# Weights-stationary products by halves with all high parts first, and 512-wide recurrence products, in a one-core transformer block

## The chip, the cores and the metric

The kernel runs on one core of one Trainium2 chip. The metric is device time in microseconds from the first to the last instruction of one execution with what lies around it; the kernel before takes 1810.07 us (median of 3 runs, 1809.61 to 1811.19).

## What is computed

One block over 256 tokens of width 2048, in fp32:

```python
mod = silu(c) @ ada_w + ada_b                  # 6 rows of 2048: sh1, sc1, g1, sh2, sc2, g2
h = rmsnorm(x, norm1_g) * (1 + sc1) + sh1
q, kc, vc, ks, vs, kw, vw, g_nsa, lx, ly, ga, gb = split(h @ w_in)
o_a = attention(...)                           # compressed, selected and window branches, gated
u = causal_dwconv(lx, conv_w, conv_b)
o_b = gelu(ly) * rg_lru(u, ...)                # gated linear recurrence over the tokens
merged = sigmoid(ga) * (o_a @ proj_a) + sigmoid(gb) * (o_b @ proj_b)
x = x + g1 * (merged @ w_out)
h = rmsnorm(x, norm2_g) * (1 + sc2) + sh2
gate, val = split(h @ ffn_up)
x = x + g2 * ((gelu(causal_dwconv(gate, ...)) * val) @ ffn_down)
out = rmsnorm(x, final_g)
```

## The kernel before

**Split products.** A product in fp32 accuracy is made of fast fp32r products. Each operand is split in a high part (rounded) and a low part (the rest), and three products are summed: high x high, high x low, low x high. Activations are kept split, `[:, 0:256]` high and `[:, 256:512]` low for the 256 tokens. Weights are streamed: a piece of 128 x 2048 (1 MB) is loaded on SP's queue into one of four `raw` buffers (`stage`), and each half of it (1024 columns) is split by `split`: ScalarE copies the high part (L107), VectorE subtracts to get the low part (L108). There are three buffers each for high and low halves, and both instructions have raised priority.

**Three product forms.** In `dense_tok` the activations are stationary and the weights move, 512 wide (L202 to L204): gates of the merge, output projections, `w_out` and the FFN's down product. In the other forms the weights are stationary. `dense_pair` gives two blocks of 128 outputs (f = 0, 1), each in a PSUM bank of its own. For each of the eight weight blocks of a half, high weights multiply the whole 512 columns of the split activations (L130), so that the bank's two halves hold high x high and high x low, and low weights then multiply the 256 high columns (L131). `reduce` (L226, VectorE) adds the bank's two halves at the end. The FFN's up products use it, 42 calls with two pieces each. `dense_pair1` keeps both blocks in one bank and issues three products of 256 columns per weight block (L184, L186, L187), which add up in place; no reduction is needed. It is used for the recurrence's inputs (8 calls, a ScalarE copy at L670 after each) and its gates (8 calls, a Gelu at L721 that reads the bank). All forms take their banks from the same four PSUM banks `d`.

**Stages.** Modulation of the first norm and the attention inputs come first (to about 290 us of the trace), then attention units interleaved with recurrence inputs (to about 480 us), the recurrence with its gates (to 597), the merge in four blocks n of 512 outputs (to 906), `w_out` (to about 985), and the FFN in two halves of 12 groups of up products and 4 down products each.

**Recurrence.** For each bt of 4, VectorE makes the convolution `u`, TensorE two small products, ScalarE two sigmoids, a tanh, an exp and a square root, VectorE the scan (L707 to L716). Then for h of 2 a gate product runs, its Gelu is written over `u` (L720, L721), multiplied by the scan's result and split into `oB` (L722 to L726).

**Modulation pieces.** The last four of the six modulation rows need 64 pieces of 1 MB. `filler(n)` takes the next n: a load into a `raw` buffer, a multiply with sum on VectorE (L233) and a small addition (L234). They are placed between the products: 2 after each recurrence input, 2 after two of the gate products, 2 after each product pair of the merge's first block and 4 after those of the other three, and 16 in the FFN.

**Order.** Every load keeps program order on SP's queue (`load`, L53). A load waits there until its buffer has been read, and whatever stands behind it on the queue waits too. The order on the engines comes from a planner that simulates the program with its own costs and priorities.

## Time and profile before

| | |
|---|---|
| median of 3 runs | 1810.07 us |
| the profiled execution | 1810.84 us, span 1809.0 us |
| TensorE busy | 1788.1 us, 99% of the span, 10344 matmuls |
| VectorE busy | 1338.8 us, 74% |
| ScalarE busy | 867.3 us, 48% |
| recurrence (480 to 597 us) | TensorE 114.9, VectorE 97.3, ScalarE 87.9 of 117 us |
| merge (597 to 830 us) | TensorE 232.4, VectorE 162.4, ScalarE 98.8 of 233 us, DMA 78% |

A line of a group names the source line, the engine, the operation, output and inputs, the number of instructions, busy time and mean duration, and the idle time of the engine before them. PE is TensorE's matmul side and PEld its weight loads, DVE is VectorE, ACT ScalarE, SPq SP's DMA queue. Matmuls are pipelined: their durations overlap, and the distance from start to start is shorter than a duration.

### The profile page before, as it was taken

Reading aid. Unit: us, or ns where it says so; the run is one execution under the profiler, and the core shown is the slowest. Engines: PE = TensorE matmul, PEld = TensorE weight load, DVE = VectorE, ACT = ScalarE, POOL = GpSimd, SP = SyncE. Lnnn points to the kernel's source line nnn. Section 1 sums busy time; section 2 is a strip of 40 time slices with the busy share of each in tenths; the row PEclk is TensorE's granted clock in tenths of the full one; section 3 lists DMA queues with packets and bytes.
Section 4 is the critical chain, followed back from the end, with each engine's and each line's share of the span. In section 5 each row is a group of like instructions: output and inputs, shape, how many; then the busy total and the mean of one; then the engine's idle time right before and its main releaser. Section 6 shows DMA issues by size and latency. Waiting matters only on the chain.

```text
span 1809.0 us, 25836 instructions
## 1 busy us (share of the span) xinstructions
PE 1788.1 (99%) x10344; PEld 1555.3 (86%) x10344; DVE 1338.8 (74%) x1942; ACT 867.3 (48%) x1176; POOL 0.2 (0%) x4
## 2 busy tenths in 40 slices
PE   8999999999999999999999999999999999999998
PEld 7899898788899888888888998888888888888886
DVE  7999866898788866767666898888555666666555
ACT  5645434655578443434445544444433444444443
POOL 0000000000000000000000000000000000000000
PEclk9999999999999999999999999999999999999999
DMA  9999862666556768787776566777655555555553
GB/s 357 366 333 361 316 245 96 214 227 210 210 175 222 273 241 292 282 285 284 294 278 209 172 231 235 277 279 279 249 190 189 188 189 189 191 190 190 186 189 113
DMA packets 64201, 429.51 MB, mean 237 GB/s; under 512 B 7089, under 2 KB 7377, under 8 KB 15569
## 3 DMA queue, kind: packets, MB, share of 16 engines
q1 hardware_dynamic: 63792, 427.08, 66.3%
q8 instruction: 81, 1.33, 0.3%
q10 hardware_dynamic: 288, 0.79, 0.1%
q14 instruction: 40, 0.32, 0.1%
HBM read 425.72 MB, written 2.11 MB: 237 GB/s over the span
## 4 chain that ended last, share of the span: by engine, by line
PE 94%; DVE 3%; DMA 1%; ACT 1%; issue 1%; DVEq 0%; ACTq 0%
PE P L130 17%; PE P L203 11%; PE P L204 11%; PE P L202 11%; PE P L131 9%; PE P L187 3%; PE P L184 3%; PE P L186 3%; PE P L426 2%; PE P L428 2%; PE P L427 2%; PE P L420 2%; PE P L421 2%; PE P L419 1%; PE P L148 1%; PE P L147 1%
## 5 line engine op out<-in xcount | busy, mean ns | idle before, releaser
L107 ACT ACTIVATE hi<-raw 128x1024 fp32r<-128x1024 f32 x589 | 623.2, 1060 | 808.9 <-PE P L204 322.0
L108 DVE TENSOR_TENSOR lo<-raw,hi 128x1024 fp32r<-128x1024 f32 x589 | 718.6, 1223 | 388.1 <-ACT hi L107 387.1
L130 PE MATMUL P<-h,hi 128*128 128x512 f32 x1344 | 465.9, 397 | 0.0
L131 PE MATMUL P<-h,lo 128*128 128x256 f32 x1344 | 362.8, 280 | 0.0
L130 PEld LDWEIGHTS P<-h,hi 128*128 128x128 f32 x1344 | 246.7, 188 | 53.2
L131 PEld LDWEIGHTS P<-h,lo 128*128 128x128 f32 x1344 | 253.6, 189 | 7.7
L233 DVE SCALAR_TENSOR_TENSOR raw<-raw,crow 128x2048 f32<-128x2048 f32 x64 | 146.3, 2286 | 13.0 <-DMA raw<-ada_w 13.0
L187 PE MATMUL P<-h,lo 128*128 128x256 f32 x512 | 147.1, 288 | 2.1 <-DVE lo L108 2.1
L184 PE MATMUL P<-h,hi 128*128 128x256 f32 x512 | 146.7, 287 | 0.0
L186 PE MATMUL P<-h,hi 128*128 128x256 f32 x512 | 146.6, 286 | 0.0
L426 PE MATMUL P<-h,hi 128*128 128x256 f32 x384 | 108.0, 286 | 0.0
L427 PE MATMUL P<-h,hi 128*128 128x256 f32 x384 | 107.3, 284 | 0.0
L428 PE MATMUL P<-h,lo 128*128 128x256 f32 x384 | 102.2, 284 | 0.0
L187 PEld LDWEIGHTS P<-h,lo 128*128 128x128 f32 x512 | 97.7, 191 | 3.9 <-DVE lo L108 2.6
L184 PEld LDWEIGHTS P<-h,hi 128*128 128x128 f32 x512 | 97.9, 191 | 3.3 <-issue 3.0
L186 PEld LDWEIGHTS P<-h,hi 128*128 128x128 f32 x512 | 97.9, 191 | 1.1 <-issue 1.0
L203 PE MATMUL P<-lo,ua 128*128 128x512 f32 x240 | 93.4, 389 | 0.0
L204 PE MATMUL P<-hi,ua 128*128 128x512 f32 x240 | 93.4, 389 | 0.0
L202 PE MATMUL P<-hi,ua 128*128 128x512 f32 x240 | 83.6, 389 | 0.0
L203 PE MATMUL P<-lo,h 128*128 128x512 f32 x192 | 75.5, 393 | 0.6 <-DVE lo L108 0.5
L204 PE MATMUL P<-hi,h 128*128 128x512 f32 x192 | 74.9, 390 | 0.0
L426 PEld LDWEIGHTS P<-h,hi 128*128 128x128 f32 x384 | 74.1, 193 | 0.2
(265 smaller groups left out, 3121.9 us busy)
## 6 DMA issues: line engine op xcount, KB each, us to landing
raw<-ada_w SPq DMA_DIRECT2D x96, 1024.0 KB, 5.0
raw<-w_up SPq DMA_DIRECT2D x96, 1024.0 KB, 4.9
raw<-w_down SPq DMA_DIRECT2D x48, 1024.0 KB, 4.9
raw<-w_lru SPq DMA_DIRECT2D x32, 1024.0 KB, 5.0
raw<-w_proj SPq DMA_DIRECT2D x32, 1024.0 KB, 5.0
raw<-w_gates SPq DMA_DIRECT2D x24, 1024.0 KB, 6.4
raw<-w_out SPq DMA_DIRECT2D x16, 1024.0 KB, 5.0
raw<-w_kv SPq DMA_DIRECT2D x24, 512.0 KB, 6.8
```

The source lines that it names most:

```text
L107: A.activation(hi[:, :n], raw[:, lo_col:lo_col + n], AF.Copy)
L108: V.tensor_tensor(lo[:, :n], raw[:, lo_col:lo_col + n], hi[:, :n].bitcast(F32), op=ALU.subtract)
L130: PE.matmul(ps[f], hi[:, sl], r, start=(kt == 0), stop=False, skip_group_check=True)
L131: PE.matmul(o, lo[:, sl], r[:, 0:256], start=False, stop=(kt == n - 1), skip_group_check=True)
L184: PE.matmul(o, hi[:, sl], r[:, 0:256], start=(kt == 0 and f == 0), stop=False, skip_group_check=True)
L186: PE.matmul(o, hi[:, sl], r[:, 256:512], start=False, stop=False, skip_group_check=True)
L187: PE.matmul(o, lo[:, sl], r[:, 0:256], start=False, stop=(kt == n - 1), skip_group_check=True)
L202: PE.matmul(ps[j], xh, hi[:, w], start=(kt == 0), stop=False, skip_group_check=True)
L203: PE.matmul(ps[j], xh, lo[:, w], start=False, stop=False, skip_group_check=True)
L204: PE.matmul(ps[j], xl, hi[:, w], start=False, stop=(kt == n - 1), skip_group_check=True)
L233: V.scalar_tensor_tensor(raw, raw, 1.0, row, op0=ALU.mult, op1=ALU.mult, accum_out=modc[:, c:c + 1])
L426: PE.matmul(o, hi[:, sl], h1[:, kt, 0:256], start=first and f % 2 == 0, stop=False, skip_group_check=True)
```

## The change

`dense_pair` now issues, for each half of a piece, the eight products with high weights first (both blocks), and then the eight with low weights. `dense_pair1` is dropped. Recurrence inputs and gates call `dense_pair` in its place: each call takes two banks, and two reductions on VectorE replace the ScalarE copy, or stand ahead of the Gelu, which now reads and writes SBUF. One modulation piece follows each recurrence input in place of two, and the eight pieces so taken out are put into the merge: 3 for 2 after each product pair of its first block, 5 for 4 after those of the other blocks.

```diff
-        def dense_pair(pieces, rhs, narrow=False):
+        def dense_pair(pieces, rhs):
...
                     hi, lo = split(raw, half * 1024, 1024)
-                    for f in range(2):
-                        for k in range(4):
...
-                                PE.matmul(ps[f], hi[:, sl], r, start=(kt == 0), stop=False, skip_group_check=True)
-                            PE.matmul(o, lo[:, sl], r[:, 0:256], start=False, stop=(kt == n - 1), skip_group_check=True)
+                    for w in (hi, lo):
+                        for f in range(2):
+                            for k in range(4):
+                                kt = ip * 8 + half * 4 + k
+                                sl = slice(k * 256 + f * 128, k * 256 + f * 128 + 128)
+                                if w is hi:
+                                    PE.matmul(ps[f], w[:, sl], rhs(kt), start=(kt == 0), stop=False,
+                                              skip_group_check=True)
+                                else:
+                                    PE.matmul(ps[f][:, 0:256], w[:, sl], rhs(kt)[:, 0:256], start=False,
+                                              stop=(kt == n - 1), skip_group_check=True)
...
         for pr in range(8):
-            pl = dense_pair1([w_lru[pr, k] for k in range(2)], h1r)
-            A.activation(lx[pr // 2][:, 2 * (pr % 2):2 * (pr % 2) + 2],
-                         pl.rearrange("p (f t) -> p f t", f=2), AF.Copy)
+            ps = dense_pair([w_lru[pr, k] for k in range(2)], h1r)
+            for f in range(2):
+                reduce(lx[pr // 2][:, 2 * (pr % 2) + f], ps[f])
             if units:
                 attention(*units.pop(0))
-            filler(2)
+            filler(1)
...
-                pl = dense_pair1([w_lru[8 + pr, k] for k in range(2)], h1r)
+                ps = dense_pair([w_lru[8 + pr, k] for k in range(2)], h1r)
                 gl = u[:, 2 * h:2 * h + 2]
-                tbl(A.activation(gl, pl.rearrange("p (f t) -> p f t", f=2), AF.Gelu_apprx_tanh))
+                for f in range(2):
+                    reduce(gl[:, f], ps[f])
+                tbl(A.activation(gl, gl, AF.Gelu_apprx_tanh))
...
-                filler(2 if n == 0 else 4)
+                filler(3 if n == 0 else 5)
```

## The prediction

> **What bounds the kernel now.** I read the page's first part, then the windows, where the tensor engine's idle time shows by stretch, and then the waits of that engine.

> ```profile
> span 1809.0 us, 25836 instructions
> PE 1788.1 (99%) x10344; PEld 1555.3 (86%) x10344; DVE 1338.8 (74%) x1942; ACT 867.3 (48%) x1176; POOL 0.2 (0%) x4
> ...
> L131 PE MATMUL P<-h,lo 128*128 128x256 f32 x1344 | 362.8, 280 | 0.0
> ...
> L184 PE MATMUL P<-h,hi 128*128 128x256 f32 x512 | 146.7, 287 | 0.0
> ```

> TensorE is busy for 1788.1 of 1809.0 us, so the time is the number of matmuls times the step from one to the next, plus the few places where it stands. The profiled execution took 1810.84 us, 1.8 us more than its span; the median of the runs shown is 1810.07 us. I work with differences and put them on the median. The mean durations (280 and 287 ns) overlap one another, so they are not steps. The steps come from stretches that hold one kind of work. These are windows of the trace (start:end, their length, TensorE's busy time and matmuls, its clock, the DMA share, GB/s), the first all in the FFN's up products, the second in its down products:

> ```profile
> 1420.00:1660.00 240.00, 240.00 (x1371) 1.00 0.55 188
> 1700.00:1780.00 80.00, 80.00 (x354) 1.00 0.56 188
> ```

> In the first, 512-wide and 256-wide products alternate: two matmuls take 2 x 240 / 1370 = 350.4 ns. In the second all are 512 wide: 80 / 353 = 227 ns (one matmul that straddles the border taken off each). The clock is full, so none of this is throttling. For 256-wide products alone, the timeline of TensorE inside one recurrence-gate product (start, duration, line):

> ```profile
> 502.03 0.28 PE L186 MATMUL P<-h,hi 128*128 128x256 f32 x1
> ...
> 505.98 0.28 PE L186 MATMUL P<-h,hi 128*128 128x256 f32 x1
> ```

> Thirty-three matmuls lie between these starts: 3.95 / 33 = 120 ns. Where TensorE waits for other engines (total us, times, longest):

> ```profile
> PE P L187 <- DVE lo L108: 2.1, 2, 1.5
> ...
> PE P L203 <- DVE lo L108: 0.5, 1, 0.5
> ```

> **The change on TensorE.** *Recurrence inputs and gates.* Sixteen calls, each of 4 halves of 8 weight blocks, did three 256-wide products per block: 24 x 120 = 2.88 us a half. They now do 8 products 512 wide and then 8 of 256. *Order in the half.* Does running equals together change the step? The planner already swaps a few, and the timeline shows both sorts of neighbour:

> ```profile
> 1200.53 0.40 PE L130 MATMUL P<-h,hi 128*128 128x512 f32 x1
> 1200.77 0.40 PE L131 MATMUL P<-h,lo 128*128 128x256 f32 x2
> 1201.01 0.40 PE L130 MATMUL P<-h,hi 128*128 128x512 f32 x1
> 1201.25 0.28 PE L131 MATMUL P<-h,lo 128*128 128x256 f32 x1
> ...
> 1202.06 0.62 PE L130 MATMUL P<-h,hi 128*128 128x512 f32 x2
> 1202.52 0.28 PE L131 MATMUL P<-h,lo 128*128 128x256 f32 x1
> ```

> A 512-wide product after a 256-wide one takes 0.24 us to the next start; two in a row take 0.46, so the second takes about 0.225, the step of the down products. Two 256-wide in a row take 0.24, 120 ns each, against 350 - 234 = 116 in alternation. So a half costs 234 + 7 x 227 + 116 + 7 x 120 = 2.78 us. In the FFN (1344 / 8 = 168 halves) it was 8 x 350.4 = 2.80: **4 us** less (168 x 23 ns). In the recurrence it was 2.88: 64 x 0.10 = **6 us** less. The other bound is that order does nothing: then FFN 0, and the recurrence 64 x (2.88 - 2.80) = 5. I take 4 and 6, since the rows of equal neighbours are the nearest.

> [...]

> **The change on VectorE and ScalarE.** 32 reductions of a 512-wide bank are added, 16 of them with the gates, and eight ScalarE copies go. The reduction exists in the FFN; the other rows are the recurrence stretch (window, then busy time of TensorE, weight load, VectorE, ScalarE) and its VectorE groups (busy, mean ns, idle before and what ended it):

> ```profile
> L226 DVE TENSOR_REDUCE gp<-P 128x256 f32<-128x512 f32 x42 | 28.2, 687 | 0.2
> ...
> 480.00:597.00 117.00, 114.94 (x884) 110.71 (x883) 97.26 (x137) 87.91 (x115) 0.00 (x0) 1.00 0.58 205
> ...
> L108 DVE TENSOR_TENSOR lo<-raw,hi 128x1024 fp32r<-128x1024 f32 x34 | 41.4, 1219 | 8.4 <-ACT hi L107 8.4
> ...
> L713 DVE SCALAR_TENSOR_TENSOR lt<-lt 128x1024 f32<-128x1024 f32 x4 | 4.9, 1225 | 8.4 <-ACT lt L711 8.4
> ```

> VectorE has 97.3 of 117 us there and gets 16 x 0.69 = 11.0 more, while the stretch shortens by 3: 108.3 of 114. Off the tensor path as long as the low parts come in time; its cover shrinks from 19.7 to 5.7 us of idle. For it speaks that a low part is now wanted only after eight high products (8 x 0.227 = 1.8 us), more than the longest wait of 1.5 us above, so up to 2.1 us of waits go. I take -1, with -2 and +8 (rival two) as ends. The gates' bank is freed by a reduction that must come after `u` is read (L712) instead of by the Gelu after the square root; that is earlier, but only two pairs of banks are left where four single ones were. The eight input calls lose eight modulation pieces of 2.3 us and gain 16 reductions, so VectorE has less to do there, and TensorE did not wait there for a low part that any row shows.

> **The moved pieces.** A piece is a 1 MB load on SP's queue into one of four `raw` slots, a 2.29 us pass of VectorE, its 0.08 us accumulator read and an addition. At each of the six places behind the merge's products for n = 1 to 3 there were four, now five; at n = 0 three for two. They stand on SP's queue ahead of the next weights, so the price is the delay of those. SP's queue (start, stretch, loads), and VectorE between (the accumulator reads that free a slot):

> ```profile
> 663.14 11.21 SPq L53 DMA_DIRECT2D raw<-ada_w  x4
> 676.23 7.09 SPq L53 DMA_DIRECT2D raw<-w_gates  x4
> ...
> 719.75 7.21 SPq L53 DMA_DIRECT2D raw<-w_gates  x4
> ...
> 764.77 7.09 SPq L53 DMA_DIRECT2D raw<-w_gates  x4
> ...
> 809.38 7.10 SPq L53 DMA_DIRECT2D raw<-w_gates  x4
> ...
> 853.62 7.09 SPq L53 DMA_DIRECT2D raw<-w_gates  x4
> ...
> 897.22 7.24 SPq L53 DMA_DIRECT2D raw<-w_out  x4
> ```

> ```profile
> 676.12 0.08 DVE L233 DVE_READ_ACCUMULATOR raw<-raw,crow 128x1 f32 x1
> ...
> 679.47 0.08 DVE L233 DVE_READ_ACCUMULATOR raw<-raw,crow 128x1 f32 x1
> ```

> The first gate weights are issued at 676.23, when the second piece's read (676.12) frees its slot. A fifth piece takes that slot, and the weights wait for the third piece's read: 679.55, **3.3 us later**. When do they land, and when are they wanted? ScalarE's high parts that waited for them, and TensorE at the first and the fourth place:

> ```profile
> 681.30 1.06 ACT L107 ACTIVATE hi<-raw 128x1024 fp32r<-128x1024 f32 x1 [3.12 <-DMA raw<-w_gates]
> ...
> 771.04 2.01 ACT L107 ACTIVATE hi<-raw 128x1024 fp32r<-128x1024 f32 x2 [4.32 <-DMA raw<-w_gates]
> 815.89 2.01 ACT L107 ACTIVATE hi<-raw 128x1024 fp32r<-128x1024 f32 x2 [5.66 <-DMA raw<-w_gates]
> 858.85 2.17 ACT L107 ACTIVATE hi<-raw 128x1024 fp32r<-128x1024 f32 x2 [3.27 <-DMA raw<-w_gates]
> 903.13 2.01 ACT L107 ACTIVATE hi<-raw 128x1024 fp32r<-128x1024 f32 x2 [2.17 <-DMA raw<-w_out]
> ```

> ```profile
> 685.08 0.62 PE L202 MATMUL P<-hi,h 128*128 128x512 f32 x2
> ...
> 817.13 0.63 PE L202 MATMUL P<-hi,h 128*128 128x512 f32 x2
> 818.26 0.51 PE L203 MATMUL P<-lo,h 128*128 128x512 f32 x1 [0.50 <-DVE lo L108]
> ```

> Landing took 681.30 - 676.23 = 5.1, then 6.3, 6.5, 5.2 and 5.9 us. High part 1.06 and low part 1.23 make 2.3 us more. At the first place the low part would be there at 679.55 + 5.07 + 2.3 = 686.9 and is wanted one step after 685.08, at 685.3: a stall of 1.6. At the fourth, 809.38 + 3.3 + 6.5 + 2.3 = 821.5 against 817.4, less the 0.7 that it stalls already (818.26 - 817.13 - two steps): 3.4. The slack that was there is thus one to two microseconds or none, and a fifth piece takes 3.3. With landings as they were, six places cost about 6 x (1.6 + 3.4) / 2 = 15; with every landing as quick as 5.1 the fourth costs 2.0 and the six about 6 x 1.7 = 10. I take **+13**. At n = 0 a third piece costs nothing: with two, gate weights go out at 626.33 for a product at 640.61, 14.3 us ahead against 8.9 at the first place above.

> ```profile
> 626.33 9.00 SPq L53 DMA_DIRECT2D raw<-w_gates  x4
> ```

> Sum: -4 - 6 - 1 + 13 = +2 us, 1812 on the median.

> **The rivals.** *One: the six places hold.* A slot comes free sooner, or the planner places the pieces so that the next weights are not behind the fifth. For it: the 8.9 us lead is more than landing and split (5.1 + 2.3 = 7.4). Against: SP's loads keep program order, and the third piece can't be read before it lands. Price of nothing: 1810.07 - 11 = 1799. *Two: VectorE becomes the bound in the recurrence.* If its idle time behind the chain of square root (8.4 us) and half of that behind the high parts (4.2) can't be filled, it needs 108.3 + 12.6 = 120.9 us in 114 and low parts come 7 us late: 1812 + 7 + 1 = 1820, slower. It decides once more than 5.7 us of idle stay. Against: VectorE works in order, but the planner lays conv and scans between. *Three: tensor work does not shrink.* Both forms stream 768 columns per block; if the step follows columns alone, 10 us of gain go and the time is 1810 + 13 - 1 = 1822. [...]

> **How the numbers follow.** The forecast that the two sides cancel has 0.5, at 1812, own range 1808 to 1816. Rival one 0.3, at 1799; rival two 0.15; rival three 0.05. What can't be told from no change is 0.2%, 3.6 us: 1806.4 to 1813.7. Of the forecast's 0.5, 0.03 lies below it, 0.36 in it and 0.11 above. Faster 0.3 + 0.03 = 0.33, same 0.36, slower 0.11 + 0.15 + 0.05 = 0.31. The range reaches into rival one and to the near end of rival two: 1798 to 1818.

> **What would show it.** Right: 512 fewer matmuls, up products at about 174 ns a matmul instead of 175, recurrence halves at 2.78 us, and six holes of 1.5 to 3.5 us at L202 or L203 behind the merge's pieces, with high parts that wait for w_gates some 3 us later than now. Wrong: no new holes there (then 1799), or TensorE waiting for low parts between the recurrence products (then above 1815). A change of the FFN's step in the other direction would break the 4 us.

## The result, and the profile after

The changed kernel takes 1835.49 us (median of four runs, 1834.41 to 1838.87) against 1809.84 us for the kernel before on the same chip: a ratio of 1.0144, 95% interval 1.0126 to 1.0161. It is slower by some 26 us, and outside the predicted range. The profiled execution took 1838.87 us, the one of before 1810.84.

The first part of the page after, and two of its groups (line, operation, count, then busy time, mean ns, idle before):

```profile
span 1837.1 us, 24842 instructions
...
PE 1797.8 (98%) x9832; PEld 1536.0 (84%) x9832; DVE 1360.7 (74%) x1974; ACT 865.6 (47%) x1172; POOL 0.2 (0%) x4
...
L129 PE MATMUL P<-h,hi 128*128 128x512 f32 x1856 | 475.9, 395 | 0.8 <-ACT hi L107 0.8
...
L132 PE MATMUL P<-h,lo 128*128 128x256 f32 x1856 | 262.7, 283 | 0.5 <-DVE lo L108 0.3
```

The 512 matmuls are gone (10344 to 9832), yet TensorE is busy for 9.7 us more, and the span has grown by 28.1. Where, by stage, from the start of the first matmul of each kind of work to that of the next, in both profiled executions:

| stage | before, us | after, us | difference |
| --- | --- | --- | --- |
| to the first attention scores | 288.4 | 289.5 | +1.1 |
| attention, inputs, recurrence, gates | 304.0 | 306.9 | +2.9 |
| merge | 308.9 | 331.9 | +23.0 |
| `w_out` | 90.9 | 94.4 | +3.5 |
| FFN | 803.1 | 800.5 | -2.6 |

Nearly all of it is in the merge and at the entry of `w_out`; the recurrence's stretch, which was to shrink by some 7 us, has grown by 2.9. TensorE's waits after (total us, times, longest); L184 to L186 are the products of `dense_tok`:

```profile
PE P L184 <- ACT hi L107: 8.8, 7, 1.9
PE P L185 <- DVE lo L108: 7.9, 8, 2.1
```

Twelve of these fifteen waits are the holes that the prediction named; the rest are in the merge's first block (n = 0). The first place, on SP's queue, in VectorE's piece reads (the third and the fifth piece), and on TensorE (start, duration, and in brackets the idle time before):

```profile
671.41 13.42 SPq L53 DMA_DIRECT2D raw<-ada_w  x5
687.85 6.03 SPq L53 DMA_DIRECT2D raw<-w_gates  x4
```

```profile
687.74 0.08 DVE L215 DVE_READ_ACCUMULATOR raw<-raw,crow 128x1 f32 x1
...
693.44 0.08 DVE L215 DVE_READ_ACCUMULATOR raw<-raw,crow 128x1 f32 x1
```

```profile
693.12 0.39 PE L186 MATMUL P<-hi,oA 128*128 128x512 f32 x1
694.56 0.73 PE L184 MATMUL P<-hi,h 128*128 128x512 f32 x2 [1.05 <-ACT hi L107]
696.05 0.50 PE L185 MATMUL P<-lo,h 128*128 128x512 f32 x1 [0.76 <-DVE lo L108]
...
697.46 0.63 PE L186 MATMUL P<-hi,h 128*128 128x512 f32 x1
697.88 0.63 PE L185 MATMUL P<-lo,h 128*128 128x512 f32 x1
```

The gate weights leave the queue when the third piece has been read (687.82), as foreseen, and TensorE waits first for a high part and then for a low one. By the starts of the matmuls (what a step lasts beyond 0.228 us, or beyond 0.427 us at half clock) the six places lose 17.4 us in all, 2.3 to 3.3 each, where 1.2 us was lost before. But the last two rows show something else: the step is now 697.88 - 697.46 = 0.42 us and not 0.227. The clock has dropped. Windows of the trace after (start:end, length, busy time and count of TensorE, weight load, VectorE, ScalarE and GpSimd, then TensorE's clock):

```profile
693.10:696.50 3.40, 1.59 (x6) 0.71 (x5) 3.40 (x8) 2.04 (x3) 0.00 (x0) 1.00 0.98 378
788.70:792.10 3.40, 1.77 (x9) 1.15 (x8) 3.40 (x8) 1.24 (x2) 0.00 (x0) 1.00 0.98 383
...
696.70:699.80 3.10, 3.10 (x9) 2.45 (x8) 1.65 (x2) 0.83 (x1) 0.00 (x0) 0.50 1.03 431
700.20:703.30 3.10, 3.10 (x15) 2.54 (x15) 1.23 (x1) 1.40 (x2) 0.00 (x0) 1.00 0.83 338
```

For 3.41 us after the hole (696.6 to 700.0) the clock is at 0.50. At a step of 0.426 us such a stretch holds 8 matmuls where full clock would hold 15, so it costs 7 x 0.228 = 1.6 to 1.7 us beside the hole. After has four of these in the merge and `w_out` (behind the first, second, fourth and sixth place), and one of twice the length at the attention's end (488.4 to 495.2 us). The kernel before has none between 23 us and its last 5 us.

The added pieces therefore cost 16.2 us of holes and 4 x 1.7 = 6.8 us of slow clock, 23.0 of the 26.5 us by which merge and `w_out` grew. Another 2.2 us is a hole at 610 us of the trace, in the merge's first projection.

### The profile page after: what moved, and what is told of

It reads as the page before. It is cut to its first block, busy times and chain, and to the rows that moved or that the text cites. A ratio compares the mean times of both kernels' runs of the same rounds, so it can differ in the third digit from the quotient of the medians.

```text
span 1837.1 us, 24842 instructions
## 1 busy us (share of the span) xinstructions
PE 1797.8 (98%) x9832; PEld 1536.0 (84%) x9832; DVE 1360.7 (74%) x1974; ACT 865.6 (47%) x1172; POOL 0.2 (0%) x4
## 4 chain that ended last, share of the span: by engine, by line
PE 82%; DVE 10%; DMA 3%; ACT 3%; issue 2%; SPq 0%; DVEq 0%; ACTq 0%
PE P L129 20%; PE P L132 10%; PE P L185 10%; PE P L186 10%; PE P L184 10%; DVE lo L108 3%; DVE raw L215 3%; PE P L408 2%; PE P L410 2%; PE P L409 2%; DMA raw<-ada_w 2%; PE P L402 2%; PE P L403 1%; PE P L401 1%; PE P L150 1%
## 5 line engine op out<-in xcount | busy, mean ns | idle before, releaser
L107 ACT ACTIVATE hi<-raw 128x1024 fp32r<-128x1024 f32 x589 | 622.0, 1060 | 823.8 <-PE P L186 307.1
L108 DVE TENSOR_TENSOR lo<-raw,hi 128x1024 fp32r<-128x1024 f32 x589 | 716.6, 1221 | 353.2 <-ACT hi L107 345.8
L129 PE MATMUL P<-h,hi 128*128 128x512 f32 x1856 | 475.9, 395 | 0.8 <-ACT hi L107 0.8
L129 PEld LDWEIGHTS P<-h,hi 128*128 128x128 f32 x1856 | 333.3, 189 | 62.5 <-issue 3.0
L132 PEld LDWEIGHTS P<-h,lo 128*128 128x128 f32 x1856 | 254.4, 191 | 21.3 <-DVE lo L108 1.5
L132 PE MATMUL P<-h,lo 128*128 128x256 f32 x1856 | 262.7, 283 | 0.5 <-DVE lo L108 0.3
L215 DVE SCALAR_TENSOR_TENSOR raw<-raw,crow 128x2048 f32<-128x2048 f32 x64 | 146.2, 2285 | 6.0 <-DMA raw<-ada_w 5.9
L408 PE MATMUL P<-h,hi 128*128 128x256 f32 x384 | 108.2, 286 | 0.0
L409 PE MATMUL P<-h,hi 128*128 128x256 f32 x384 | 107.6, 284 | 0.0
L410 PE MATMUL P<-h,lo 128*128 128x256 f32 x384 | 102.1, 284 | 0.0
L185 PE MATMUL P<-lo,ua 128*128 128x512 f32 x240 | 93.4, 389 | 0.0
L186 PE MATMUL P<-hi,ua 128*128 128x512 f32 x240 | 93.4, 389 | 0.0
L184 PE MATMUL P<-hi,ua 128*128 128x512 f32 x240 | 83.6, 389 | 0.0
L185 PE MATMUL P<-lo,h 128*128 128x512 f32 x192 | 77.9, 406 | 4.1 <-DVE lo L108 4.1
L186 PE MATMUL P<-hi,h 128*128 128x512 f32 x192 | 77.2, 402 | 0.0
L184 PE MATMUL P<-hi,h 128*128 128x512 f32 x192 | 68.8, 398 | 7.8 <-ACT hi L107 7.8
L408 PEld LDWEIGHTS P<-h,hi 128*128 128x128 f32 x384 | 74.2, 193 | 0.2
L409 PEld LDWEIGHTS P<-h,hi 128*128 128x128 f32 x384 | 74.2, 193 | 0.0
L304 DVE SCALAR_TENSOR_TENSOR raw<-raw,crow 128x2048 f32<-128x2048 f32 x31 | 70.7, 2283 | 1.2 <-DMA raw<-ada_w 1.1
L410 PEld LDWEIGHTS P<-h,lo 128*128 128x128 f32 x384 | 70.6, 192 | 0.8 <-issue 0.8
L150 PE MATMUL P<-hp,hi 128*128 128x258 f32 x192 | 53.9, 283 | 0.0
L149 PE MATMUL P<-hp,hi 128*128 128x258 f32 x192 | 53.4, 283 | 0.0
```

What stands on the lines that cost most here:

```text
L107: A.activation(hi[:, :n], raw[:, lo_col:lo_col + n], AF.Copy)
L108: V.tensor_tensor(lo[:, :n], raw[:, lo_col:lo_col + n], hi[:, :n].bitcast(F32), op=ALU.subtract)
L129: PE.matmul(ps[f], w[:, sl], rhs(kt), start=(kt == 0), stop=False, skip_group_check=True)
L132: PE.matmul(ps[f][:, 0:256], w[:, sl], rhs(kt)[:, 0:256], start=False, stop=(kt == n - 1), skip_group_check=True)
L150: PE.matmul(o, hi[:, sl], r[:, 1], start=False, stop=False, skip_group_check=True)
L184: PE.matmul(ps[j], xh, hi[:, w], start=(kt == 0), stop=False, skip_group_check=True)
```

## The experiments

The chip was not always the same, so each kernel is given by its ratio to the kernel before run beside it, and by that ratio times 1810 us. In the names, a *place* is one of the merge's six positions of moved pieces for n = 1 to 3.

**Each part alone.** The changed kernel with the old placing of the pieces (e1), and the kernel before with the new placing (e2):

```diff
--- the changed kernel
+++ e1
-            filler(1)
+            filler(2)
-                filler(3 if n == 0 else 5)
+                filler(2 if n == 0 else 4)
--- the kernel before
+++ e2
-            filler(2)
+            filler(1)
-                filler(2 if n == 0 else 4)
+                filler(3 if n == 0 else 5)
```

> The changed kernel with the modulation pieces where they were (2 after each recurrence input, 2 and 4 in the merge). Theory P (the moved pieces alone cost the time: six holes of 2.1 to 3.4 us, three smaller ones in the merge's first block, and a tensor clock that falls to half behind them): all of the merge's 23 us and most of w_out's 3.5 go, and the recurrence gains its 6, about 1803 us, clock 0.998. Rival F (the 512-wide form costs too, since its two banks a call leave the end of the attention uncovered): the merge is repaired but the recurrence stays some 8 us above what the products need, about 1811 us.

> The kernel before with nothing but the eight pieces moved. Theory P: the holes do not depend on the product forms, so six holes, four clock windows at half speed and 1809.8 + 23 + 2 = about 1835 us. Rival F: holes that need the reductions' load on VectorE too; then less than half of that, below 1822 us.

e1: 1813.79 us, ratio 1.0014 [1.0005, 1.0023], +2.5 us. e2: 1837.39 us, ratio 1.0133 [1.0115, 1.0150], +24.1 us. The placing of the pieces costs about 24 us by itself, with or without the new products (e1 to after: 23.5). TensorE's waits of e2 in the same notation, where L202 and L203 are `dense_tok`:

```profile
PE P L203 <- DVE lo L108: 7.6, 8, 1.5
PE P L202 <- ACT hi L107: 5.7, 6, 1.9
```

And the part that should have gained leaves a small loss. Its two halves, the order of products in the FFN's calls (e3) and with it the gate calls alone in the new form (e7):

```diff
--- e3 (the kernel before with dense_pair as in the change, dense_pair1 kept)
+++ e7
-                pl = dense_pair1([w_lru[8 + pr, k] for k in range(2)], h1r)
+                ps = dense_pair([w_lru[8 + pr, k] for k in range(2)], h1r)
...
-                tbl(A.activation(gl, pl.rearrange("p (f t) -> p f t", f=2), AF.Gelu_apprx_tanh))
+                for f in range(2):
+                    reduce(gl[:, f], ps[f])
+                tbl(A.activation(gl, gl, AF.Gelu_apprx_tanh))
```

> The kernel before with only the order inside the up products changed (all high weights of a half first). The trace after shows 230 ns for a 512-wide product in a run of eight and 120 for a 256-wide one, 2.80 us a half against 2.80 to 2.81 before: 0 to 3 us less, 1807 to 1810 us. My prediction's step of 4 us would give 1806.

> e3_order_only with the eight gate calls alone in the 512-wide form on two banks (reductions into u, as the change has it); the eight input calls stay 256 wide on one bank, and the merge is the old one. It prices the gates' half of the recurrence by itself. If a gate call saves its 32 x 0.10 us, 1806 to 1807; if the banks wait for u, 1811 to 1814; the difference to e1 (1813.8) is then what the input calls cost.

e3: 1809.42 us, ratio 0.9985 [0.9977, 0.9994], -2.7 us. e7: 1806.22 us, ratio 0.9968 [0.9956, 0.9980], -5.8 us, the fastest kernel of the study. So order is worth 2.7 us, within 1.5, and the gates in the new form 3.1 more, within 2.7 (from the intervals). The window of e3 that answers the first one of the prediction:

```profile
1420.00:1660.00 240.00, 240.00 (x1377) 211.22 (x1376) 167.07 (x234) 103.14 (x118) 0.00 (x0) 1.00 0.56 189
```

240 / 1376 = 174.4 ns for a matmul, against 175.2 before. What is left between e7 (-5.8) and e1 (+2.5) is the eight input calls: they *cost* 8.3 us, within 2.7.

**The price of the pieces: placing, and the clock.** With the pieces of a place divided, two behind the gate products and three behind the projections (e4), or eight products with an unused result put into each of the six holes of the changed kernel (e5; `tail[0]` is the last projection product):

```diff
--- the changed kernel
+++ e4
                     ps = dense_tok([w_gates[n - 1, s, k] for k in range(4)], h1r)
+                    filler(2)
...
-                filler(3 if n == 0 else 5)
+                filler(3)
--- the changed kernel
+++ e5
...
+        def cover():
+            o = psx.tile([128, 512], F32, tag="o", bufs=1, name="cover")
+            with tc.issue_after(tail[0].ins):
+                for _ in range(8):
+                    PE.matmul(o, oA[:, 0, 0:128], oA[:, 0, :], start=True, stop=True, skip_group_check=True)
...
+                if n > 0:
+                    cover()
```

> The changed kernel with the same pieces in the merge, but 2 behind the gate products and 3 behind the projections instead of 5 in a row. Theory P by bunching (a fifth piece in a row takes the slot that the next weights would have): the holes go, although as many bytes and VectorE passes lie in the merge, so 1803 to 1811 us. Rival L (the merge can't take 42 pieces at all, VectorE or DMA being full): it stays above 1825 us.

> The changed kernel with eight additional 512-wide products (their result unused) ahead of the weights that come late, at each of the six places in the merge: 6 x 8 x 0.227 = 10.9 us of work put into holes of 2.1 to 3.4 us. Theory C (the drops of the tensor clock behind the holes are part of the price, 3.4 us at half speed or 1.7 us lost each time): the holes are filled, the four clock windows of the merge stay away and the time falls by some 5 to 7 us, to about 1829, although work is added. Rival N (the clock has nothing to do with the holes, or the drops cost nothing): the time stays or rises, 1835 or more.

e4: 1815.22 us, ratio 1.0020 [1.0010, 1.0029], +3.6 us: the holes at the six places are gone and with them 22 us, though it moves the same pieces. It isn't the number of pieces that costs, but five in a row ahead of the next weights. TensorE's waits in `dense_tok` in e4, of which the long one is the hole at n = 0:

```profile
PE P L185 <- DVE lo L108: 2.0, 1, 2.0
...
PE P L184 <- ACT hi L107: 0.3, 1, 0.3
```

e5: 1832.47 us, ratio 1.0112 [1.0097, 1.0127], +20.3 us. It does 48 x 0.227 = 10.9 us more tensor work than the changed kernel, and is 5.8 us *faster* (1.0144 - 1.0112, times 1810; the intervals touch). Its weights are as late as before: the six places still lose 6.7 us by the starts of the matmuls, and with the 10.9 us of added products that is 17.6, where the changed kernel lost 17.4. What is gone from the merge and `w_out` is the slow clock; four windows are 6.8 us. The merge of after and of e5 (the clock is the number behind the five busy times):

```profile
597.00:906.00 309.00, 294.16 (x1279) 238.72 (x1279) 221.81 (x245) 128.56 (x139) 0.00 (x0) 0.98 0.76 284
```

```profile
597.00:906.00 309.00, 302.48 (x1343) 247.35 (x1342) 223.82 (x249) 132.04 (x144) 0.00 (x0) 1.00 0.77 289
```

**The recurrence: shared tiles.** In the changed kernel the reductions of input calls 6 and 7 (counted from 0; calls 8 to 15 are the gates'), whose products ended on TensorE at 465.1 and 479.1 us, ran only at 490:

```profile
488.15 1.87 PE L629 MATMUL oT<-pcT,cmpb 15*128 15x512 f32 x2
```

```profile
490.06 2.48 DVE L208 TENSOR_REDUCE lx<-P 128x256 f32<-128x512 f32 x4
```

Their destination shares a tile with `cmpb`, which the last attention unit still reads. The two calls hold all four banks, so call 8 can't begin and the attention's end has nothing beside it. In e6 `kcmp` and `vcmp` have tiles of their own; e9 is e6 with divided pieces:

```diff
--- e1
+++ e6
-        kcmp = cmpb[:, 256:316]
-        vcmp = cmpb[0:16, 316:828]
...
+        kcmp = tmp.tile([128, 256], F32, tag="rB", bufs=1, name="kcmp")[:, 0:60]
+        vcmp = [tmp.tile([128, 256], F32, tag="xp", bufs=2, name="vcmp") for _ in range(2)]
...
--- e6
+++ e9
                     ps = dense_tok([w_gates[n - 1, s, k] for k in range(4)], h1r)
+                    filler(2)
...
-                filler(2 if n == 0 else 4)
+                filler(2)
```

> The kernel of e1_old_pieces with the compressed keys and values of attention in other buffers (those of rB1 and xp), so that the last recurrence inputs no longer share a tile with them. Theory B (their four reductions wait for the last attention unit's read of that tile, and the two calls hold all four PSUM banks till then): the next products fill the end of attention, the hole of 2.9 us and both half-speed clock windows near 480 us go, 5 to 8 us less than e1_old_pieces, about 1806 to 1809. Rival D (VectorE's load or the latency of attention makes the hole): it stays within 2 us of e1_old_pieces.

> Hi-first order, 512-wide recurrence products, attention's compressed values in buffers of their own, old number of pieces with 2 and 2 in the merge: what both theories call the best of each. By P, B and bunching together 1809.8 - 3 (order) - 5 (recurrence products) - 1 (merge) + what is left of the holes inside the recurrence (up to 4) = 1801 to 1805.

e6: 1817.72 us, ratio 1.0037 [1.0024, 1.0049], +6.7 us. e9: 1816.55 us, ratio 1.0026 [1.0015, 1.0037], +4.7 us. The hole at the attention's end is gone, as expected, but the time is no better. Holes have come up later:

```profile
PE P L132 <- DVE lo L108: 3.8, 3, 2.4
...
PE P L129 <- DVE lt L208: 2.5, 2, 2.2
PE P L129 <- ACT hi L107: 2.5, 1, 2.5
```

Among them are gate calls whose banks (L208) wait for `u`. So the reductions of the gates got a tile of their own, in e6 (e10), in e9 (e12) and in e1 (e11):

```diff
-                gl = u[:, 2 * h:2 * h + 2]
+                if h == 0:
+                    gt = lx[bt] if bt < 3 else big.tile([128, 4, T], F32, tag="D0", name="gt")
+                gl = gt[:, 2 * h:2 * h + 2]
```

> e6_own_vcmp with one more edit: the two reductions and the Gelu of a gate call go into the buffer of the input values that this batch no longer needs (a free one for the last batch), not into u, so that a gate call's two banks are emptied as soon as its products end and not after u's last reader. Theory W (banks held by a reduction that waits for its destination): in e6 calls 8, 9 and 12 waited up to 18 us for u; with that gone the holes of 2.7, 1.3, 2.7 and 2.5 us between 527 and 577 us go and the time is 1805 to 1811. Rival V (VectorE is full there: 97 us and more of work, with the added reductions, in a stretch of some 107 us, and the low parts are late): the holes stay within 2 us in sum and the time is 1815 to 1819.

> e10_own_gates with the merge's moved pieces as two behind each pair of gate products and two behind each pair of projections for n = 1 to 3, as in e8. The pieces' placing gave e4 no holes in the merge; so theory W expects 1803 to 1809, under the kernel before, and rival V 1813 to 1818, as e9 (1816.6).

> e1_old_pieces with the gate calls' reductions out of u, as in e10, but kcmp and vcmp left where they share a tile with the input values. Theory W: the hole at the attention's end stays (2.9 us with two half-speed windows), the recurrence's own holes (1.97, 1.84 and 1.73 us) go, 1808 to 1812. Rival V: 1812 to 1816, no change against e1 (1813.8).

e10: 1814.34 us, ratio 1.0017 [1.0008, 1.0025], +3.1 us. e12: 1814.27 us, ratio 1.0010 [1.0001, 1.0018], +1.8 us. e11: 1816.15 us, ratio 1.0026 [1.0016, 1.0037], +4.7 us. Against e6 and e9 the new tile is worth 3.6 and 2.9 us; against e1 it is a loss of 2.2, within the noise of the two. No version with the new input calls comes below the kernel before; the shared tiles hold the products up in the trace, but taking them away did not gain back the loss.

**The recurrence: what the input calls cost.** Three suspects were left: the sixteen reductions on VectorE, the second bank that a call holds, and the 512-wide products themselves. e13 takes the reductions away and keeps bank and products; e15 keeps the old products on one bank and adds the reductions; e18 has the second bank and neither of the others. e13 copies only the first half of each bank, by ScalarE, and so leaves out the product with the low part of the activations; e15 adds two halves that hold different outputs, and leaves out the outputs themselves. These two are for time alone.

```diff
--- e10
+++ e13
-                reduce(lx[pr // 2][:, 2 * (pr % 2) + f], ps[f])
+                A.activation(lx[pr // 2][:, 2 * (pr % 2) + f], ps[f][:, 0:256], AF.Copy)
--- e7
+++ e15
-            A.activation(lx[pr // 2][:, 2 * (pr % 2):2 * (pr % 2) + 2],
-                         pl.rearrange("p (f t) -> p f t", f=2), AF.Copy)
+            for f in range(2):
+                reduce(lx[pr // 2][:, 2 * (pr % 2) + f], pl)
--- e7
+++ e18
-            p = bank()
+            ps = [bank(), bank()]
-                        o = p[:, f * 256:f * 256 + 256]
+                        o = ps[f][:, 0:256]
...
-            A.activation(lx[pr // 2][:, 2 * (pr % 2):2 * (pr % 2) + 2],
-                         pl.rearrange("p (f t) -> p f t", f=2), AF.Copy)
+            for f in range(2):
+                A.activation(lx[pr // 2][:, 2 * (pr % 2) + f], ps[f][:, 0:256], AF.Copy)
```

> e10_own_gates with the sixteen reductions of the eight input calls taken off VectorE: each bank's first half alone is copied by ScalarE (128x256), so the second half of each sum is left out and the values differ; products, banks and waits for destinations stay. Theory VA (the reductions of 0.68 us, some 10 us in the attention's stretch, push the attention and the convolutions back, and the recurrence then lacks the time): the attention ends near 484 us again instead of 510, the holes between 527 and 581 us go, 1804 to 1808. Theory B (two banks held by each input call make the rest wait): no change, 1812 to 1816.

> The converse, on e7_gates_512: the input calls keep their 256-wide products on one bank, but ScalarE's copy of each is replaced by two VectorE reductions over the whole bank (sums of the wrong halves, so the values differ; the length and number are those of the change). Theory VA: it becomes slower than e7 (1806.2) by 4 to 8 us, 1810 to 1814. Theory B: within 2 us of e7, 1805 to 1808.

> e7_gates_512 with each of the eight input calls on two banks (one for each block of outputs, the first half of each used, copied by ScalarE) but still in 256-wide products. It separates what e13 left together. Theory B (the second bank): 1811 to 1816, as e13. Theory O (the 512-wide products: the planner's order puts some 20 us more of dense products ahead of the attention's last units, which then end at 510 us instead of 484; with two banks alone its order stays that of e7): attention ends at 484, 1805 to 1808.

e13: 1814.70 us, ratio 1.0016 [1.0007, 1.0025], +2.9 us. e15: 1808.57 us, ratio 0.9984 [0.9975, 0.9993], -2.9 us. e18: 1808.10 us, ratio 0.9974 [0.9964, 0.9984], -4.7 us. Beside e7 (-5.8) the reductions cost some 3 us and the second bank about 1, which is within the noise, while e13, without the reductions, has the whole loss of e10. What e13 and e10 share and the others lack is the 512-wide products in the input calls, and beside them the tiles that were moved in e6 and e10. No run has the moved tiles with 256-wide inputs; but e1, with 512-wide inputs and the old tiles, loses as much (+2.5), in part by the hole of the shared tile.

Their profiles differ from e7's in the same way. VectorE's convolution steps (count at the end of the shape) done between 293 and 480 us in e7, e15 and e18, one fence each, and then in e10 and e13:

```profile
L699 DVE SCALAR_TENSOR_TENSOR lt<-lx,cols,lt 128x253 f32<-128x253 f32 (+2 forms) x24 | 10.7, 474 | 0.0
```

```profile
L699 DVE SCALAR_TENSOR_TENSOR lt<-lx,cols,lt 128x253 f32<-128x253 f32 (+2 forms) x24 | 10.7, 476 | 0.0
```

```profile
L699 DVE SCALAR_TENSOR_TENSOR lt<-lx,cols,lt 128x253 f32<-128x253 f32 (+2 forms) x24 | 10.9, 476 | 0.0
```

```profile
L680 DVE SCALAR_TENSOR_TENSOR lt<-lx,cols,lt 128x253 f32<-128x253 f32 (+2 forms) x12 | 5.5, 471 | 0.0
```

```profile
L680 DVE SCALAR_TENSOR_TENSOR lt<-lx,cols,lt 128x253 f32<-128x253 f32 (+2 forms) x15 | 7.0, 476 | 0.0
```

And the recurrence's two windows in e7 and e10:

```profile
480.00:530.00 50.00, 50.00 (x282) 43.05 (x281) 38.01 (x55) 36.07 (x49) 0.00 (x0) 1.00 0.55 191
530.00:597.00 67.00, 66.76 (x374) 58.43 (x373) 64.11 (x92) 52.88 (x67) 0.00 (x0) 1.00 0.63 228
```

```profile
480.00:530.00 50.00, 47.90 (x253) 38.99 (x252) 35.19 (x65) 33.41 (x51) 0.00 (x0) 1.00 0.46 169
530.00:597.00 67.00, 63.09 (x341) 54.35 (x340) 65.04 (x97) 51.09 (x70) 0.00 (x0) 0.97 0.56 198
```

In e10 and e13 the attention's last products stand at 510 and 507 us instead of 484, twelve and nine of these 24 convolution steps come after 480, and TensorE is busy for 5 to 6 us less in the two windows. In the program's instruction order, counted at 0.23 us for a 512-wide product and 0.12 for a 256-wide one, 23 us more of dense products than in e7 stand ahead of the compressed branch of the last attention unit in e10, 20 more in e13, 12 more in e1 and none more in e18. So in the 512-wide form the planner puts 12 to 23 us more of dense work ahead of the attention's end. That the planner counts this form as cheaper than the chip runs it would explain it, but that is only argued, and so is the step from the late attention to each later hole. In e15 the attention's last products stand at 496 and its order has 7 us more, with 24 convolution steps before 480 and a small loss.

**A version from the parts that paid.** Divided pieces on e3 (e8) and on e7 (e17); in e14 the second `filler(2)` stood by mistake in the branch of n = 0:

```diff
--- e3, e7
+++ e8, e17
                     ps = dense_tok([w_gates[n - 1, s, k] for k in range(4)], h1r)
+                    filler(2)
...
-                filler(2 if n == 0 else 4)
+                filler(2)
```

> The kernel of e3_order_only with the merge's four pieces in a row put as 2 behind the gates and 2 behind the projections. If bunching is what delays the next weights, the two small stalls that are left in the merge (0.3 and 0.7 us) and the longer steps behind them go: 1 to 2 us less than e3_order_only. If four in a row cost nothing: the same as e3_order_only.

> A version made of the parts that paid: e7_gates_512 with the merge's pieces two behind each pair of gate products and two behind each pair of projections, as e8 has them. e8's merge gained 2.4 us on e3's; if that holds here 1803 to 1806, else e7's 1806.

> The version from the parts that paid: e7_gates_512 with the merge's pieces for n = 1 to 3 as two behind each pair of gate products and two behind each pair of projections (e14 was meant to be this, but its second pair stood in the branch of n = 0, which left twelve pieces over behind the merge, queued on VectorE ahead of the merge's last sum). 1803 to 1807.

e8: 1808.22 us, ratio 0.9981 [0.9972, 0.9990], -3.4 us. e14: 1827.81 us, ratio 1.0092 [1.0078, 1.0106], +16.7 us. e17: 1806.63 us, ratio 0.9969 [0.9957, 0.9982], -5.6 us, level with e7. Dividing gains nothing beyond the noise on e3 (0.7 us) or on e7; both e7 and e17 beat both kernels of the case. By its code e14 leaves eight pieces over (not twelve, as e17's expectation has it), and they were queued on VectorE behind the merge. A count of VectorE's groups in e14 between 893 and 928 us, and TensorE's waits:

```profile
L235 DVE SCALAR_TENSOR_TENSOR raw<-raw,crow 128x2048 f32<-128x2048 f32 x10 | 22.8, 2284 | 0.0
```

```profile
PE turn L765 <- DVE sg L760: 6.7, 2, 4.5
...
PE turn L765 <- DVE mg L768: 4.2, 1, 4.2
```

Ten pieces, 22.8 us of VectorE, have the merge's last sum (L760) and the transposes behind it waiting among them, and the clock is at 0.50 in the whole window from 912 to 925 us. As in the change a long run of pieces delays what stands behind it, here on VectorE's queue and not on SP's.

## Why the prediction was wrong, point by point

The forecast was -4 -6 -1 +13 = +2. The runs give four terms that can be set beside it (e3, e7 less e3, e1 less e7, after less e1; the total is the ratio of the changed kernel):

| step | foreseen, us | measured, us |
| --- | --- | --- |
| order in the FFN | -4 | -2.7 |
| gates 512 wide | -3 | -3.1 |
| inputs 512 wide, and waits for low parts | -3 -1 | +8.3 |
| moved pieces | +13 | +23.5 |
| sum | +2 | +26.1 |

- *The moved pieces, the first step that failed, by size.* The mechanism was right in each link: the fifth piece takes the slot, the weights wait for the third piece's read, a hole opens at L184 and L185 at each of six places, 2.3 to 3.3 us where 1.5 to 3.5 was foreseen. The holes lost 16.2 us more than before against the 13 taken, a little over the upper bound of 15. (The lower bound is 6 x 1.8 = 11 by the rows it was worked out from, not 10.) What the sum left out is the clock. "The clock is full, so none of this is throttling" was read from the profile before, and then held for a kernel with holes, where it no longer is: four stretches at half clock, 6.8 us. e5 takes those away and gains 5.8 us in spite of 10.9 us more of work. Holes and clock together are 23.0 us, and the runs give 23.5 for the pieces.
- *n = 0 costs nothing.* A hole of 2.2 us is there at 610 us. e1, with the new products and the old two pieces, has one of 1.5 us at 609, and e2, with the old products and three pieces, one of 0.8 us at 610 and one of 0.5 at 599; before there is none. So the third piece does cost something there, the new products more.
- *The recurrence's -6 and -1, the second step that failed, by sign for one half.* Priced by steps of TensorE the gates came out right to a tenth, which is luck where the runs tell it only within 2.7 us. For the inputs the step is nearly as short as foreseen (an unbroken half takes 2.79 us, where 2.78 was foreseen and 2.88 measured before), and the gain is lost many times over. "VectorE has less to do there" looked at VectorE's sum. The reductions do cost 3 us (e15), but 512-wide products among attention units come with another interleaving, the attention's end and the convolutions come later, and TensorE waits in the recurrence; how the one leads to the other stays open. In the changed kernel itself the loss stands at the attention's end, by the shared tile: there "only two pairs of banks left" was written down and given no price.
- *The order in the FFN.* Of 4 us, 2.7 came, and the interval (1.1 to 4.2) holds both. By the trace it is nearer 2: a 512-wide product in a run of equals steps by 230 ns in the changed kernel, not by the 227 of the down products, and a half takes 2.79 us and not 2.78, so that 168 halves gain 168 x 12 ns. The sign was right, and with it that order matters at all.
- *The rivals.* One (the places hold) fell: all six opened. Three (the work does not shrink) fell with e3 and e7. Two (VectorE becomes the bound in the recurrence, 1820) had the right place: VectorE is busy for 65 of 67 us at the stretch's end. But e7 has 64.1 us there, and e13, without the inputs' reductions, 65.2, and they differ by 8.7 us, so that VectorE's load is not what decides.
- *The range.* Its upper end of 1818 was rival two alone. The case that pieces and recurrence both go wrong was not in it, though no reason excluded it.

## What to carry to other kernels

In the changed kernel's trace a hole on a full TensorE cost its own length (2.3 to 3.3 us) and, at four of six places, 1.7 us of slow clock more: price a foreseen hole with both, and a fill-in of unused products can even pay (5.8 us in e5). Work that is hung into gaps, like the modulation pieces, is priced by what stands behind the longest run of it on its queue, not by its amount: four in a row lost 1.2 us, five cost 24 more, and the same number divided in two cost 1 of that, within the noise. And where an order planner stands between code and chip, a change that shortens the products of a stretch with latency-bound work beside it (the attention here) is tried by itself before it is counted as a gain.

## What the runs showed of the hardware

With the raster carried on through the trace, and idle time worked out from the starts of the matmuls (a step longer than 0.24 us counts as idle beyond it), the windows at full clock after the attention (from 500 us to the last matmul) that were idle to 0.67, 0.86, 0.73 and 0.77 (at 693.2, 741.0, 836.6 and 932.1 us) were followed by half clock; the others idle to 0.30 or more, with 0.52 (788.8 and 884.3 us), 0.46 (611.3) and 0.42 (792.2), were not, nor was the one of 0.45 in the trace before (562.2). What happens between 0.52 and 0.67 these two traces do not show. The windows shown above are an example: 1.59 us busy of 3.40 at 693.1 is followed by half clock, 1.77 of 3.40 at 788.7 is not, although the place there loses more (3.3 us against 2.3), for its hole lies across two windows. So in these traces it mattered how a hole fell on the raster. The mean clock also changes from run to run: e2's profiled run took 1831.67 us at a mean clock of 0.995, and its three other runs are 5 to 7 us longer at 0.992 to 0.993, where one stretch takes 0.0009 off the mean (3.41 x 0.50 / 1830). That their holes fell differently on the raster was not shown.

At the attention's end the same count does not decide: half clock came after a window idle to 0.50 (485.0 us in the trace after), less than the 0.52 that had none behind it at 788.8, and it went on for a second window after a slow one idle to 0.33 only (488.4 us, steps to 0.45 us taken as full there). What decides among the small products was not settled.
